# Input projection of a four-branch decoder layer: one Strassen level over blocks of 1024 tokens, columns passed on through DRAM

## The chip, the core and the metric

The kernel runs on one core of one Trainium2 chip. The metric is the device time of one execution in microseconds (us); three runs of the kernel before gave a median of 2729.23 us (2728.61 to 2731.78).

## The reference

One layer of a decoder on 2048 tokens of width 1024, all in float32:

```python
h = _rmsnorm(x, norm_pre)
cols = h @ w_in                      # (2048 x 1024) @ (1024 x 9992)
(dn_qkv, dn_z, dn_b, dn_a, gm_uv, gm_z, sw_q, sw_k, sw_v, sw_z, xm_q, xm_z, gate_logits) = _split_cols(cols)
mem_kv = _rmsnorm(mem, norm_mem) @ w_mem_kv
y_a = _deltanet_branch(dn_qkv, dn_z, dn_b, dn_a, ...)   # conv, silu, chunked delta rule with a state that runs over the tokens
y_b = _spatial_gating_branch(gm_uv, gm_z, ...)          # gelu, 128x128 mixing of positions
y_c = _sliding_window_branch(sw_q, sw_k, sw_v, sw_z, sinks)
y_m = _memory_branch(xm_q, xm_z, mem_kv)                # attention to 256 memory tokens
proj = jnp.einsum("btnc,ncd->btnd", jnp.stack([y_a, y_b, y_c, y_m], axis=2), w_up)
merged = jnp.sum(jax.nn.sigmoid(gate_logits.reshape(B, T, 4, D)) * proj, axis=2)
return x + _rmsnorm(merged @ w_out, norm_post)
```

Of the 9992 columns of the projection 8 belong to the two small gates of the DeltaNet branch; the other 9984 are 78 tiles of 128 columns (32 of them gate logits).

## The kernel before

**Products.** Each float32 matrix is split into a high part (rounded to fp32r, a cast on ScalarE) and a low part (the difference, a subtraction on VectorE or GpSimd); a product is three matmuls, high by high, low by high and high by low (`mac3`, L259). A matmul has 128 rows, 128 columns and 512 tokens.

**Passes.** The tokens go through in four passes of 512 (`for p in range(NPASS)`, L1146). In a pass the normalised input `hhi`, `hlo` (L350) stays in SBUF. Two tiles of 128 columns at a time are projected by `proj2` (L264): two units of weights (512 KB each) are loaded, split (`wunit`, L228) and multiplied, 48 matmuls in all. The result is taken from PSUM by the branch that wants it, at once: it never leaves SBUF.

**Order of the work.** The program is written with generators. A foreground generator (`fg`, L105) projects or multiplies; at each of its `yield`s every background generator (`start`, L114) goes one step. So the emission of the slow chains is spread over the foreground: `proj2` yields every 12 matmuls. The compiler then orders the instructions of each engine by readiness with the emission order as priority; buffers with one tag are handed out in the order of the program.

**The DeltaNet chain.** `dn_step` (L593) and `dn_scan` (L732) run per pass and per pair of heads (`q` = 0, 1): norms of keys and queries, the 32x32 triangular systems written to DRAM and read back in another layout (L661, L669), their solution by 32 pairs of a multiplication and a reduction on VectorE (L675, L676), written out and read back (L683, L686), the assembly of the 128x128 inverses, and a scan over four chunks in which each needs the state `S` of the one before. It has two PSUM buffers of its own (`dnp`, L80). Eight such chains run, each in the background of a good part of a pass's projections: chain 0 beside `branch_b`, `branch_c_kv`, `branch_c_q` and `gates_up(1)`, chain 1 beside `gates_up(2)` and others.

**The up projection.** `gates_up(n)` (L422) projects the 8 gate tiles of branch n, multiplies the branch's output by `w_up[n]` and adds the gated product to `merged`. After the fourth, `out_proj` (L1074) multiplies by `w_out`; the next pass's `phase_h` (L463) runs beside it.

Of the kernel before, what the change touches and what calls it, by code (L numbers as in the profile page):

```python
# [20 lines left out]
NB = TB // P  # L21
H = 4
EPS = 1e-6
NW, NWR = 6, 3
NS = 7
NT, NC, ND, NE = 12, 4, 11, 6
# [11 lines left out]
def trunk(tc, x, mem, norm_pre, norm_post, norm_mem, w_in, conv_w, a_log, dt_bias, dn_norm,  # L38
# [4 lines left out]
    NPASS = x.shape[0] // TB  # L43
# [5 lines left out]
    hp = pool("h", 1)  # L49
    wp = pool("w", 3)  # L50
# [3 lines left out]
    dp = pool("scr", 2, space=DRAM)  # L54
# [4 lines left out]
    def ctmp(name, dt=F32):  # L59
        return tp.tile([P, 512], dt, name=name, tag="c", bufs=NC)  # L60

    def dtmp(name, dt=F32):
        return tp.tile([P, 512], dt, name=name, tag="d", bufs=ND)

    def etmp(name, dt=F32):
        return tp.tile([P, 256], dt, name=name, tag="e", bufs=NE)

    def junk():
        return tp.tile([P, 512], BF16, name="junk", tag="e", bufs=NE)
# [15 lines left out]

    def load_rows(src, name, tmp):
        xt = [tmp(f"{name}x{i}") for i in range(2)]
        for i in range(2):
            nc.sync.dma_start(xt[i], src[:, i * 512:(i + 1) * 512])
        return xt  # L90

    first_rows = [load_rows(x[t * P:(t + 1) * P], "x", dtmp) for t in range(NB)]


# [10 lines left out]
    def fg(gen):  # L105

        try:
            while True:
                next(gen)
                step()  # L110
        except StopIteration as e:
            return e.value
# [26 lines left out]
    def wait(n):  # L139
        for _ in range(n):  # L140
            yield


# [21 lines left out]
    sel = cp.tile([P, 4, 4], F32R, name="sel")  # L165
    sel_f = small("sel_f", 16)
    V.memset(sel_f, 1.0)
    G.affine_select(sel_f.rearrange("p (i j) -> p i j", i=4), sel_f.rearrange("p (i j) -> p i j", i=4),
                    [[1, 4], [-1, 4]], ALU.is_equal, 0.0, base=0, channel_multiplier=0)
    V.tensor_copy(sel, sel_f.rearrange("p (i j) -> p i j", i=4))  # L170
# [22 lines left out]
    inv = cp.tile([P, 8, P], F32, name="inv")  # L193
    ud4 = dp.tile([4, 8, 32], F32, name="ud4", tag="ud4", bufs=1)


    def late_constants():
# [17 lines left out]
        tc.keep_in_program_order(G.memset(inv, 0.0))  # L215
# [9 lines left out]
    nsplit, solving = [0], []  # L225
    ON_DVE = ("gu", "gv", "gz", "az", "xq", "xz", "gate0", "gate2", "gate3", "u0", "u2", "u3", "wo")

    def wunit(src, name, k=4, swap=False, tags=None):  # L228


        raw = wp.tile([P, 1024], F32, name=f"{name}raw", tag="wraw", bufs=NWR)
        for d, s in (src if isinstance(src, list) else [(slice(None), src)]):
            nc.sync.dma_start(r3(raw, k)[d], s)
        res = []
        pl, th, tl, bufs = tags or (wp, "whi", "wlo", NW)
        for i in range(2):
            hi = pl.tile([P, 512], F32R, name=f"{name}hi", tag=th, bufs=bufs)
            lo = pl.tile([P, 512], F32R, name=f"{name}lo", tag=tl, bufs=bufs)
            rw = raw[:, i * 512:(i + 1) * 512]
            nsplit[0] += 1  # L240
            eng = V if name in ON_DVE or nsplit[0] % 3 == 0 and not solving else G
            if swap:
                perm = lambda t: t.rearrange("p (k a b c) -> p k b a c", k=2, a=2, b=2)
                same = lambda t: t.rearrange("p (k a b c) -> p k a b c", k=2, a=2, b=2)
                for kk in range(2):
                    A.copy(same(hi)[:, kk], perm(rw)[:, kk])
                    eng.tensor_tensor(same(lo)[:, kk], perm(rw)[:, kk], same(hi)[:, kk].bitcast(F32), op=ALU.subtract)
            else:
                A.copy(hi, rw)  # L249
                ins = eng.tensor_tensor(lo, rw, hi.bitcast(F32), op=ALU.subtract)  # L250
                if nsplit[0] < 5:
                    tc.keep_in_program_order(ins)
            res.append((r3(hi, k // 2), r3(lo, k // 2)))
        return lambda j: (res[j // (k // 2)][0][:, j % (k // 2)], res[j // (k // 2)][1][:, j % (k // 2)])
# [4 lines left out]
    def mac3(ps, lh, ll, rh, rl, first, last):  # L259
        T.matmul(ps, lh, rh, start=first, stop=False)  # L260
        T.matmul(ps, lh, rl, start=False, stop=False)  # L261
        T.matmul(ps, ll, rh, start=False, stop=last)  # L262

    def proj2(src, name, done, rh=None, rl=None, n=TB, swap=False):  # L264

        rh, rl = (hhi, hlo) if rh is None else (rh, rl)
        pss = [mm(name), mm(name)]
        for j in range(2):
            unit = wunit(src(j), name, swap=swap)
            for i in range(2):  # L270
                for k in range(4):
                    hi, lo = unit(k)
                    kk = 4 * j + k
                    mac3(pss[i][:, :n], hi[:, i * P:(i + 1) * P], lo[:, i * P:(i + 1) * P], rh[:, kk], rl[:, kk],
                         kk == 0, kk == KT - 1)
                if j:
                    done(i, pss[i])
                yield

    def cols_of(w, col):  # L280
        v = kview(w[:, col:col + 2 * P])
        return lambda j: v[:, 4 * j:4 * j + 4]
# [953 lines left out]
```

## Time and profile before

| | |
|---|---|
| median of three runs | 2729.23 us |
| profiled execution | 2728.63 us, span 2726.9 us |
| TensorE (PE) busy | 2684.6 us, 98% |
| VectorE (DVE) busy | 1546.7 us, 57% |
| ScalarE (ACT) busy | 1105.2 us, 41% |
| GpSimd (POOL) busy | 682.2 us, 25% |
| DMA | 271.29 MB, 34% of 16 engines' time |

The span goes from the first to the last instruction of the profiled execution. Matmuls are pipelined: each is recorded for longer than the distance to the next one, so the busy time of PE says that matmuls were in flight, and the distance of two starts says what one costs.

### The profile page before, as it was taken

What the parts mean: (1) busy time and instruction counts of PE and PEld (TensorE: products, weight loads), DVE (VectorE), ACT (ScalarE), POOL (GpSimd) and SP (SyncE); (2) the same over time, 40 slices, a digit from 0 to 9 for tenths busy, and PEclk for the clock granted to TensorE, in tenths of its full rate; (3) what the DMA queues carried; (4) which work ended last, traced back from release to release, by engine and by line L of the source; (5) the groups of instructions that cost most, each with busy time, mean ns of one, the idle gap of its engine ahead of it and who ended that gap; (6) DMA issues with size and microseconds to landing.
All of it is one profiled execution on the core that took longest, in us unless ns stands there. A gap on an engine that the chain in (4) does not pass through costs nothing. (4 is left out here: it accounts for less than half of the span.)

```text
span 2726.9 us, 37167 instructions
## 1 busy us (share of the span) xinstructions
PE 2684.6 (98%) x13453; PEld 2176.5 (80%) x13453; DVE 1546.7 (57%) x3355; ACT 1105.2 (41%) x2484; POOL 682.2 (25%) x689
## 2 busy tenths in 40 slices
PE   7989999999999999999999999999999999999998
PEld 5868777888888877888878887788887877778887
DVE  7464377544557547754465656665447455675444
ACT  5524343334453444343444334434344443433332
POOL 3333322011224332101223433210113334221111
PEclk9989999999999999999999999999999999999999
DMA  4342333224433233323533323332343332333242
GB/s 136 103 118 86 93 93 86 85 85 137 143 89 104 76 93 87 100 70 93 170 102 94 104 78 85 103 91 71 108 155 116 88 96 74 89 95 89 78 123 93
DMA packets 268015, 271.29 MB, mean 99 GB/s; under 512 B 33264, under 2 KB 238648, under 8 KB 267832
## 3 DMA queue, kind: packets, MB, share of 16 engines
q1 hardware_dynamic: 267656, 268.89, 34.1%
q8 instruction: 106, 1.74, 0.3%
q14 instruction: 77, 0.63, 0.1%
q10 hardware_dynamic: 80, 0.03, 0.0%
q0 software_dynamic: 96, 0.01, 0.0%
HBM read 251.31 MB, written 12.06 MB: 97 GB/s over the span
## 5 line engine op out<-in xcount | busy, mean ns | idle before, releaser
L455 POOL TENSOR_TENSOR merged<-merged,gp 128x512 f32<-128x512 f32 x96 | 138.7, 1445 | 685.2 <-DVE gp L454 670.4
L675 DVE TENSOR_TENSOR pr<-L,U 128x8 f32<-128x8 f32 (+31 forms) x256 | 102.0, 398 | 44.2 <-DMA L<-scr 37.4
L431 ACT ACTIVATE gt<-gate 128x512 f32<-128x512 f32 x128 | 76.2, 595 | 122.1 <-PE gate L262 121.8
L260 PE MATMUL gate<-hhi,gate1hi 128*128 128x512 f32 x256 | 105.9, 414 | 0.0
L260 PE MATMUL gate<-hhi,gate2hi 128*128 128x512 f32 x256 | 102.3, 400 | 0.0
L260 PE MATMUL wo<-wohi,mh 128*128 128x512 f32 x256 | 102.0, 399 | 0.0
L260 PE MATMUL gate<-hhi,gate3hi 128*128 128x512 f32 x256 | 100.8, 394 | 0.0
L261 PE MATMUL gate<-hlo,gate1hi 128*128 128x512 f32 x256 | 100.5, 393 | 0.0
L262 PE MATMUL gate<-hhi,gate1lo 128*128 128x512 f32 x256 | 100.5, 393 | 0.0
L262 PE MATMUL wo<-wohi,ml 128*128 128x512 f32 x256 | 100.0, 391 | 0.0
L261 PE MATMUL gate<-hlo,gate2hi 128*128 128x512 f32 x256 | 100.0, 391 | 0.0
L261 PE MATMUL gate<-hlo,gate3hi 128*128 128x512 f32 x256 | 100.0, 391 | 0.0
L260 PE MATMUL gate<-hhi,gate0hi 128*128 128x512 f32 x256 | 99.9, 390 | 0.0
L262 PE MATMUL gate<-hhi,gate2lo 128*128 128x512 f32 x256 | 99.9, 390 | 0.0
L262 PE MATMUL gate<-hhi,gate3lo 128*128 128x512 f32 x256 | 99.8, 390 | 0.0
L261 PE MATMUL wo<-wolo,mh 128*128 128x512 f32 x256 | 99.6, 389 | 0.0
L261 PE MATMUL gate<-hlo,gate0hi 128*128 128x512 f32 x256 | 99.6, 389 | 0.0
L262 PE MATMUL gate<-hhi,gate0lo 128*128 128x512 f32 x256 | 99.6, 389 | 0.0
L250 DVE TENSOR_TENSOR gate0lo<-gate0raw,gate0hi 128x512 fp32r<-128x512 f32 x64 | 44.0, 692 | 94.7 <-ACT gate0hi L249 94.7
L454 DVE SCALAR_TENSOR_TENSOR gp<-gt,up 128x512 f32<-128x512 f32 x96 | 65.6, 683 | 54.0 <-PE up L262 53.2
L250 POOL TENSOR_TENSOR gate1lo<-gate1raw,gate1hi 128x512 fp32r<-128x512 f32 x48 | 62.1, 1301 | 125.8 <-ACT gate1hi L249 125.7
L250 DVE TENSOR_TENSOR gate3lo<-gate3raw,gate3hi 128x512 fp32r<-128x512 f32 x64 | 44.3, 692 | 81.7 <-ACT gate3hi L249 81.7
(483 smaller groups left out, 8272.8 us busy)
## 6 DMA issues: line engine op xcount, KB each, us to landing
gate1raw<-in_w_in_dram SPq DMA_DIRECT2D x32, 512.0 KB, 3.6
gate2raw<-in_w_in_dram SPq DMA_DIRECT2D x32, 512.0 KB, 3.6
gate3raw<-in_w_in_dram SPq DMA_DIRECT2D x32, 512.0 KB, 3.6
gate0raw<-in_w_in_dram SPq DMA_DIRECT2D x32, 512.0 KB, 3.7
woraw<-in_w_out_dram SPq DMA_DIRECT2D x32, 512.0 KB, 3.8
xx<-in_x_dram SPq DMA_DIRECT2D x32, 256.0 KB, 5.1
dn0raw<-in_w_in_dram SPq DMA_DIRECT2D x16, 512.0 KB, 3.6
dn1raw<-in_w_in_dram SPq DMA_DIRECT2D x16, 512.0 KB, 3.7
```

What stands on the lines that cost most here:

```text
L250: ins = eng.tensor_tensor(lo, rw, hi.bitcast(F32), op=ALU.subtract)
L260: T.matmul(ps, lh, rh, start=first, stop=False)
L261: T.matmul(ps, lh, rl, start=False, stop=False)
L262: T.matmul(ps, ll, rh, start=False, stop=last)
L431: A.activation(t, ps, AF.Tanh, scale=0.5)
L454: V.scalar_tensor_tensor(g, ts[d2], 1.0, ps, op0=ALU.add, op1=ALU.mult)
L455: G.tensor_tensor(merged[:, d], merged[:, d], g, op=ALU.add)
L675: V.tensor_tensor(pv, L[:, i, i:32].unsqueeze(1).broadcast_to([P, 8, n]), U[:, :, i:32], op=ALU.mult)
```

## The change

**Blocks.** The tokens go through in two blocks of 1024 (`BLK`), each of two sub-blocks `s` of 512. A product of the block's input (two halves of tokens by two halves of the 1024 inputs) and of a *quad* of weights (two halves of the inputs by two tiles of 128 columns) is one level of Strassen's scheme in Winograd's form: seven products of halves where there were eight. There are 39 quads a block; a product of halves is 4 `mac3`, 12 matmuls.

**Left operands.** `phase_h` makes the transposed, scaled input of both sub-blocks, four sums of its quarters on POOL, and the split of seven operands (A11, A12, A22, S1 to S4), which take 56 buffers of 128x512 for the whole projection of a block. There is now one tag of 77 such buffers for nearly everything.

**Weights.** `Weights.load` reads four quarters (256 KB each, rows of 512 B) two quads ahead, `sums` makes four sums on POOL, and `split` splits one of seven operands two products ahead.

**Results.** The four outputs of a quad are put together from four PSUM banks by one copy (ACT) and five additions (DVE), pass through their first function (tanh, gelu, silu, or the convolution and silu of the DeltaNet's columns) and are written to a DRAM scratch (`put`). The branches, which start when all 39 quads of a block are done, read them back (`get`).

**After the projection.** `branch_b`, the DeltaNet chains (now `dn_chain`, the four of a block one after the other), the sliding window and the memory attention are the background of `up(1)`, `up(2)` and `up(3)` alone, which yield every 6 matmuls. `up(0)` and `out_proj` follow once the chains are finished. The weights `w_up` are loaded and split once a block. In the very last half of `out_proj` the weights are loaded three times.

**Smaller edits.** Row sums of squares of keys and queries by one fp32 matmul, not two of fp32r; softmax of the memory branch scaled on ACT, not on DVE; gMLP's `v` transposed on PE, as it comes with the columns on partitions; the second sub-block's rows of `x` wait for four buffers of their own tag; every other weight split outside the projection on POOL.

```diff
+NT, NX = 77, 4
...
+    def phase_h(b, gts):
+        L = {n: [None] * 4 for n in ("A11", "A12", "A22", "S1", "S2", "S3", "S4")}
...
+                for n, u, v, op in (("S1", "A21", "A22", ALU.add), ("S3", "A11", "A21", ALU.subtract),
+                                    ("S2", "S1", "A11", ALU.subtract), ("S4", "A12", "S2", ALU.subtract)):
...
+                    G.tensor_tensor(t, val(u), val(v), op=op)
...
+    def put(name, s, t):
+        nc.sync.dma_start(cols[name][:, s * TB:(s + 1) * TB], t)
...
+    class Weights:
...
+        def sums(self):
+            B11, B12, B21, B22 = self.r
+            t1, t2, t4 = (r3(tmp(n), 4) for n in ("T1", "T2", "T4"))
+            G.tensor_tensor(t1, B12, B11, op=ALU.subtract)
+            G.tensor_tensor(t2, B22, t1, op=ALU.subtract)
+            G.tensor_tensor(t4, B21, t2, op=ALU.subtract)
+            G.tensor_tensor(B12, B22, B12, op=ALU.subtract)
...
+    PRODUCTS = (("X", "A11", "B11"), ("Y", "S2", "T2"), ("W", "S3", "T3"), ("Z", "S1", "T1"),
+                ("X", "A12", "B21"), ("Z", "S4", "B22"), ("W", "A22", "T4"))
+    AHEAD = 2
+    def project(b, left, quads, ws):
...
+            bank = (lambda i: mm(f"q{i}")) if q % 2 == 0 else (lambda i: (att if i < 2 else dnp)(f"q{i}"))
...
+            for i, (p, a, w) in enumerate(PRODUCTS):
...
+                for k in range(4):
+                    ah, al = left[a][k]
+                    mac3(ps[p], hi[:, k], lo[:, k], ah, al, new and k == 0, k == 3, not new)
+                if i == 0 and q + 2 < len(ws):
+                    ws[q + 2].load()
+                if i == 3 and q + 1 < len(ws):
+                    ws[q + 1].sums()
+                q_, i_ = (q, i + AHEAD) if i + AHEAD < 7 else (q + 1, i + AHEAD - 7)
+                if q_ < len(ws):
+                    ws[q_].split(PRODUCTS[i_][2])
+                if i == 0:
+                    e1 = tmp("e1")
+                    A.copy(e1, ps["X"])
+                elif i == 1:
+                    u2 = tmp("u2")
+                    V.tensor_tensor(u2, ps["Y"], e1, op=ALU.add)
+                elif i == 3:
+                    u4 = tmp("u4")
+                    V.tensor_tensor(u4, ps["Z"], u2, op=ALU.add)
+                    o = sink.place(1, 1)
+                    V.tensor_tensor(o, ps["W"], u4, op=ALU.add)
+                    sink.done(1, 1, o)
...
+    def dn_chain(b, gts):
+        for s in range(SB):
+            for q in range(2):
+                p = b * SB + s
+                st = yield from dn_load(p, q, gts[s])
+                yield from dn_step(st)
+                on_of[p, q] = st
...
+    for b in range(NBLK):
...
+        fg(project(b, left, quads, ws))
...
+        cb = start(chain_b())
+        dn = start(dn_chain(b, gts))
+        cc = start(chain_c(b, yc))
+        finished(cb)
+        fg(up(b, 1, merged, yb))
+        finished(cc)
+        cm = start(chain_m(b, ym))
+        ca = start(chain_a(b, dn, ya))
+        fg(up(b, 2, merged, yc))
+        finished(cm)
+        fg(up(b, 3, merged, ym))
+        finished(dn, ca)
...
+        fg(up(b, 0, merged, ya, out_split))
...
+        for s in range(SB):
+            if b + 1 < NBLK and s == 1:
+                hb = start(phase_h(b + 1, gts))
+            fin = fg(out_proj(b * SB + s, mh[s], ml[s]))
```

## Rows read from the trace of the kernel before

**Rows 1.** The page, busy time, share and instructions of each engine.
```profile
PE 2684.6 (98%) x13453; PEld 2176.5 (80%) x13453; DVE 1546.7 (57%) x3355; ACT 1105.2 (41%) x2484; POOL 682.2 (25%) x689
```
**Rows 2.** Timeline of PE in a projection: start us, us recorded, line and operation.
```profile
2201.70 0.39 PE L261 MATMUL sz<-hlo,szhi 128*128 128x512 f32 x1
...
2205.80 0.39 PE L261 MATMUL sz<-hlo,szhi 128*128 128x512 f32 x1
```
**Rows 3.** Timeline of PE at the start: first transposes, first matmul of a projection.
```profile
8.34 1.11 PE L342 MATMUL xtp<-ident,xx 128*128 128x128 f32 x4 [8.34 <-DVE xx L328]
...
23.56 0.40 PE L260 MATMUL dn<-hhi,dn0hi 128*128 128x512 f32 x1
```
**Rows 4.** Groups of instructions, DVE: count, busy us, mean ns, idle before.
```profile
L675 DVE TENSOR_TENSOR pr<-L,U 128x8 f32<-128x8 f32 (+31 forms) x256 | 102.0, 398 | 44.2 <-DMA L<-scr 37.4
L676 DVE TENSOR_REDUCE U<-pr 128x8 f32<-128x8 f32 (+31 forms) x256 | 74.4, 291 | 6.9
L454 DVE SCALAR_TENSOR_TENSOR gp<-gt,up 128x512 f32<-128x512 f32 x96 | 65.6, 683 | 54.0 <-PE up L262 53.2
L250 DVE TENSOR_TENSOR gate3lo<-gate3raw,gate3hi 128x512 fp32r<-128x512 f32 x64 | 44.3, 692 | 81.7 <-ACT gate3hi L249 81.7
...
L542 DVE SCALAR_TENSOR_TENSOR dn0a<-dn,ccol,dn0a 128x509 f32<-128x509 f32 (+2 forms) x48 | 35.6, 741 | 35.9 <-ACT dn0a L539 35.4
...
L954 DVE COPY_PREDICATED sc<-gt_mask,scp 128x256 f32<-128x256 uint32 x60 | 23.9, 442 | 35.2 <-ACT sc L953 35.2
...
L1030 DVE TENSOR_REDUCE xm<-xs 128x2 f32<-128x512 f32 x32 | 21.9, 685 | 11.2 <-PE xs L262 11.0
...
L753 DVE SCALAR_TENSOR_TENSOR R<-ks,neg_eg,dv 128x128 f32<-128x128 f32 x64 | 19.4, 345 | 6.8 <-PE ks L750 5.9
...
L773 DVE SCALAR_TENSOR_TENSOR S<-S,eg,sps 128x128 f32<-128x128 f32 x64 | 19.3, 343 | 23.6 <-PE sps L770 23.5
```
**Rows 5.** Groups of instructions, POOL and ACT.
```profile
L250 POOL TENSOR_TENSOR gate1lo<-gate1raw,gate1hi 128x512 fp32r<-128x512 f32 x48 | 62.1, 1301 | 125.8 <-ACT gate1hi L249 125.7
...
L637 POOL TENSOR_TENSOR gtri<-triu,gr 128x256 fp32r<-128x256 f32 x64 | 49.8, 803 | 79.2 <-PE dps L642 51.4 <-DVE gr L531 25.6 <-DVE gr L532 2.1
...
L249 ACT CAST gate3hi<-gate3raw 128x512 fp32r<-128x512 f32 x64 | 39.9, 624 | 57.8 <-PE gate L261 42.3 <-PE az L261 9.6 <-DVE gate3lo L250 5.9
```
**Rows 6.** One chain, second of eight, by stage: busy us in each stretch, clock, DMA.
```profile
388.00:429.00 41.00, 40.46 (x225) 31.40 (x224) 24.60 (x56) 15.80 (x45) 10.74 (x16) 1.00 0.32 94
429.00:437.00 8.00, 8.00 (x42) 6.75 (x41) 5.99 (x15) 2.65 (x10) 2.43 (x2) 1.00 0.44 132
437.00:466.00 29.00, 29.00 (x128) 23.26 (x128) 27.29 (x75) 9.61 (x18) 3.17 (x3) 1.00 0.30 74
466.00:475.00 9.00, 9.00 (x59) 7.24 (x59) 4.18 (x8) 2.31 (x4) 1.29 (x1) 1.00 0.61 158
475.00:493.00 18.00, 18.00 (x155) 14.19 (x150) 10.97 (x15) 6.57 (x13) 4.70 (x3) 1.00 0.31 88
493.00:537.00 44.00, 44.00 (x244) 37.87 (x244) 24.95 (x62) 16.36 (x46) 2.10 (x3) 1.00 0.26 74
```
**Rows 7.** A stretch in which PE waited, and the two after it (columns as in Rows 6).
```profile
170.00:180.00 10.00, 3.11 (x13) 1.93 (x11) 6.35 (x13) 3.43 (x8) 4.56 (x4) 0.78 0.81 227
180.00:190.00 10.00, 9.92 (x88) 6.57 (x89) 3.04 (x8) 2.73 (x7) 1.41 (x2) 0.50 0.29 88
190.00:200.00 10.00, 10.00 (x52) 8.36 (x51) 2.03 (x6) 0.58 (x1) 0.00 (x0) 0.53 0.20 52
```
**Rows 8.** DMA: a queue's share of 16 engines, and issues with KB and us to landing.
```profile
q1 hardware_dynamic: 267656, 268.89, 34.1%
...
gate1raw<-in_w_in_dram SPq DMA_DIRECT2D x32, 512.0 KB, 3.6
xx<-in_x_dram SPq DMA_DIRECT2D x32, 256.0 KB, 5.1
...
L<-scr SPq DMA_DIRECT2D x8, 512.0 KB, 4.9
```

More of the change, by code (lines that the diff above doesn't have):

```diff
@@ L53, in trunk @@
     pp = pool("ps", 1, space=PSUM)
-    dp = pool("scr", 2, space=DRAM)
+    dp = pool("scr", 1, space=DRAM)
     def tmp(name, dt=F32):
@@ L110, in fg, with run @@
                 step()
+        except StopIteration as e:
+            return e.value
+    def run(gen):
+        try:
+            while True:
+                next(gen)
         except StopIteration as e:
@@ L518, in dn_gates @@
                         nexpa.unsqueeze(1).broadcast_to([P, NB, H]), op=ALU.mult)
-        for _ in range(9):
-            yield
+        yield from wait(2)
         gps = dnp("gps")
@@ new lines, in chain_a, with branch_b, rows @@
+    def chain_a(b, dn, ya):
+        for s in range(SB):
+            for q in range(2):
+                while (b * SB + s, q) not in on_of:
+                    yield
+                yield from branch_a(b * SB + s, q, ya[s])
+    def branch_b(b, s, ys):
+        gvt = [get(("gv", i, b), s) for i in range(4)]
+        vs = [None] * NB
+        yield
+        def rows(t):
+            tps = att("gvt")
+            for i in range(4):
+                T.transpose(tps[:, i * P:(i + 1) * P], gvt[i][:, t * P:(t + 1) * P], ident)
@@ new lines, in rows, with mix @@
+            yield
+            A.activation(vs[t], tps, AF.Copy, scale=r)
+            yield
+        yield from staggered([rows(t) for t in range(NB)], 1)
+        def mix(g):
+            u, sz = get(("gu", g, b), s), get(("gz", g, b), s)
+            sps = att("gs")
+            for c in range(NB):
+                T.matmul(sps[:, c * P:(c + 1) * P], vs[c][:, g * P:(g + 1) * P], wsT[:, g], start=True, stop=True)
+            G.tensor_tensor(sz, sz, u, op=ALU.mult)
+            yield
+            V.scalar_tensor_tensor(r3(u, NB), r3(sps, NB), g_gm[:, g:g + 1],
+                                   bsb[:, g * P:(g + 1) * P].unsqueeze(1).broadcast_to([P, NB, P]),
+                                   op0=ALU.mult, op1=ALU.add)
+            yield
+            V.tensor_tensor(u, u, sz, op=ALU.mult)
+            yield
+            ys.append(ysplit(u, "yb"))
@@ L972, in block @@
             G.tensor_tensor(scv, scv, den.unsqueeze(2).broadcast_to([P, 4, P]), op=ALU.mult)
-            yield from wait(4)
+            yield from wait(2)
             tps = att("ptp")
@@ L980, in block @@
             V.tensor_tensor(r3(prv, 4), r3(tps, 4), slow.unsqueeze(1).broadcast_to([P, 4, P]), op=ALU.mult)
-            yield from wait(2)
+            yield
             cv = cur.rearrange("p (i a q) -> p a i q", i=2, a=2)
@@ L1074, in out_proj, with chain_m @@
-    def out_proj(p, merged, mh, ml):
+        ys.append(ysplit(sz, "ym"))
+    def chain_m(b, ym):
+        t = {}
+        for n in mks:
+            t[n] = tmp("mk" + n, F32 if n[0] == "v" else F32R)
+            nc.sync.dma_start(t[n].bitcast(F32), mks[n])
+        yield from wait(2)
+        kv = ([t[f"h{h // 2}"][:, (h % 2) * MEM:(h % 2 + 1) * MEM] for h in range(H)],
+              [t[f"l{h // 2}"][:, (h % 2) * MEM:(h % 2 + 1) * MEM] for h in range(H)], [t["v0"], t["v1"]])
+        for s in range(SB):
+            for h in range(H):
+                yield from branch_m(b, s, h, kv, ym[s])
@@ new lines, in finish @@
+            for half in range(2):
+                nc.sync.dma_start(out[rows, half * 512:(half + 1) * 512], xs[t][half])
+    quads = quad_list()
+    nc.sync.dma_start(bar, kview(w_in[:, OFF_BA:OFF_BA + 8]), allow_slow_non_contiguous=True)
+    A.copy(baw[:, :, 0:8], bar)
+    V.tensor_tensor(baw[:, :, 8:16], bar, baw.bitcast(F32)[:, :, 0:8], op=ALU.subtract)
+    lc = start(late_constants())
+    gts = [{}, {}]
+    hb = start(phase_h(0, gts))
+    fg(mem_kv())
+    left = finished(hb)
+    finished(lc)
```

977 lines of the change are left out of this document (456 added, 521 removed).

## The prediction

> **What bounds the kernel now.** I read the page's busy shares first: TensorE is busy 98% of the span, DVE 57%, ACT 41%, POOL 25% [rows 1]. Then the timeline of PE, since a busy PE need not be a full one: in a projection 18 matmuls of 512 tokens take 4.10 us, 0.228 us each, with no gap [rows 2]. The reader is to see that PE is the bound nearly everywhere: 7488 such matmuls are the projection (78 tiles x 24 x 4 passes), 1536 the up projection and 768 `out_proj`, together 9792 x 0.228 = 2233 us; the rest of PE's 2684.6 us, 452 us, is the branches' small work and the transposes, and 42 us of the span are idle. Last I read one DeltaNet chain stage by stage [rows 6]: it takes 149 us, in which PE is busy 148.5 us, mostly with projections. The chain is long, but hidden.
>
> **The saving.** Seven products of halves for eight: 39 quads x 84 matmuls x 2 blocks = 6552, where there were 7488. 936 x 0.228 = 213 us of PE.
>
> **The projection of a block.** 3276 x 0.228 = 747 us, if PE stays the bound. Beside a quad's 19.2 us of PE stand 7 splits and 5 additions on DVE, 12 x 0.69 = 8.3 us (by the split of gate3lo, [rows 4]); a DeltaNet quad adds 12 multiply-adds of the convolution at 0.74 (L542, [rows 4]) and 4 for its silu, 8.9 + 2.8 = 11.6 us more, 19.9 in all, just over PE's, but there are 6 among 39 and what they leave over is worked off in the next quad. ACT has 7 casts, a copy and 4 first functions, 12 x 0.62 = 7.4 us [rows 5], and POOL 4 sums of 1.3 us, 5.2 us [rows 5]. All of it lies beside PE. Two waits are new on PE: the sixth product adds onto a bank that DVE must have read after the fourth, so DVE has one product, 2.7 us, for it, and what is queued before it on DVE are splits of 0.69 us. On SP's queue each `put` waits for its result and holds back the weights behind it, which have a quad's time to spare. The buffers are tight: of 77, 56 are held by the left operands, and the 28 allocations of a quad hold 18.6 on average (lifetimes counted in products from the diff), where 21 are free. I add 8 us a block for late splits (0 to 30): 755 us. DMA: 4 weight quarters are as many bytes per quad as before per pair of tiles and pass, 82 MB less in all, `w_up` 17 less; the columns add 82 MB each way: 268.89 becomes some 334 MB, and the 34.1% [rows 8] some 42%. No bound.
>
> **After the projection.** Here is what the change moves. The branches had the whole pass as cover; now what runs beside a block's four chains is `up(1)` to `up(3)`, 576 matmuls, 131 us, and the branches' own PE work, at most 452 / 2 = 226 us, I take 200: 331 us a block. The chains run one after the other, as they share two PSUM buffers and the state; `up(0)` and `out_proj` wait for the last. Call this stretch W. Three things bound it:
>
> PE: 331 us. DVE: the lines of the chain sum to 355 us (19 lines; the solve's two are 102.0 + 74.4, the scan's R and S 19.4 + 19.3 [rows 4]), the window attention 182 (from L954, 23.9 [rows 4], down), the memory attention 68 (from L1030, 21.9 [rows 4], down), gMLP and the output of A 66, `up` 83 (two thirds of L454 [rows 4], the first sum, 24 splits): 754, a block's half 377 us. The chains: 4 times one.
>
> One chain before takes 41 us for norms and triangular systems, 8 for their way through DRAM (the load alone lands in 4.9 us [rows 8]), 29 for the solve, 9 for the way back, 18 for the inverses, 44 for the scan [rows 6]. That is an upper bound, for it was paced by the foreground: some 60 steps, each behind 12 matmuls (2.7 us). From below: the solve's busy time, 176.4 / 8 = 22 us [rows 4]; the two DMA trips, 8 + 6 us, stay; the first stage has 10.7 us of POOL in that row, twice that with what comes before and after, 21; the inverses are half copies and waits, 9; a chunk of the scan needs two of R, two of S (4 x 0.34 [rows 4]) and three rounds of small matmuls with a hand-over each, some 4.5 us, 18 in all. Sum 84 us. Between 84 and 149 I take 110: the solve at 29 and the DMA trips at 17 as they were, since DVE will be over 80% busy and the trips don't change, and the remaining 103 us down to 64, because a step now stands behind 6 matmuls (1.4 us) and not 12, but behind a fuller DVE. So W = 440 us a block (from 377, DVE's bound, to 4 x 149 = 596). PE is idle about 110 us of it. That is the price: 2 x 110 us, as large as the saving. The next thing late is DVE.
>
> **Start, change of block, end.** Before, the first projection began at 23.6 us [rows 3]. Now 1024 tokens have to be there: rows of the second sub-block wait for four buffers until the first is transposed (some 27 us), land 12 us later (an estimate from 5.1 us per 256 KB load [rows 8], several at once), 6 us for norms, then four rounds of 10 DVE operations of 0.69, 28 us: 75 us (60 to 95), in which PE has the memory keys. At the change of block the same four rounds stand behind an `out_proj` that covers most of it: 15 us (5 to 30). The end, three loads of the last weights: 10 us, where it was some 7. `up(0)` and `out_proj` follow W: 192 + 384 matmuls, 131 us a block, and 12 us before them for the last chain's output, its transposes and splits.
>
> **The sum.** 75 + 2 x (755 + 440 + 12 + 131) + 15 + 10 = 2776 us of span; the profiled execution before was 1.7 us over its span and 0.6 us under the median of the runs. Forecast 2778 us, 1.8% slower. Its own range, chains of 104 to 125 us: 2730 to 2900.
>
> The smaller edits have one answer: fp32 squares, `v`'s transposes, the halved loads of `w_up`, splits moved to POOL, softmax scaling on ACT move a few us between engines of which, in W, only DVE counts, and are in its 377 us.
>
> **Rivals.** *The chains are hidden, PE or DVE bounds W.* For it: the minima sum to 84 us, 4 x 84 = 336 < 377; and DVE can run nearly full (27.29 of 29 us in the solve's row [rows 6]). Against: the one chain read took 149 us, and DVE would have to be full for 377 us while the chain's hand-overs, each waiting for the one before, go through it. W = 377 to 405 gives 2652 to 2708, point 2670; with PE the bound (331) 2560.
>
> *The clock.* Where PE had been busy for 3.11 of 10 us, the granted clock of the next 20 us was 0.50 and 0.53, half of 2.4 GHz [rows 7]. In W PE has work for 75% of the time and gaps at each DMA trip and solve. Four chains with two such gaps each, 20 us at half clock each, lose 8 x 10 = 80 us of PE's work a block; 110 us of W are idle anyway, but the chains' own small matmuls and what is queued before them slow down too. It decides if the clock falls at each of these gaps, as it did there, and what is lost falls on the chains' path. W = 440 + 80: 2938. The Trainium skill, "TensorE: Matmul & The Clock Gate", section "Part 1: The HAM clock gate", says that half rate is the default and only activity lifts it. The trace agrees as far as it goes: after that one gap 0.5. By that rule alone a W at half clock throughout would be PE's, 2 x 331 = 662 us, and the kernel 3220 us; a PE that is then full would get its clock back, so I give it no more than this rival's chance.
>
> *The change doesn't do what it says:* the 21 free buffers or the one-product deadline on DVE hold PE up once a quad by one product, 2.7 us: 78 x 2.7 = 213 us, all that was saved. Speaks for it that 21 against 18.6 leaves little; against it that splits are two products ahead. 2776 + 197 = 2975.
>
> **Chances.** Forecast 0.45, hidden chains 0.33, clock 0.10, held up in the projection 0.07; the seam between the first two, where W = 413 to 418 and nothing can be told from no change (0.2%, 5.5 us, is what a measurement of this kernel can tell), 0.05. So faster 0.33, same 0.05, slower 0.62. The range, 2610 to 2940, leaves out the fully PE-bound W below and the worst of the last two above.
>
> **What would show it.** In the profile after: PE full in the projection's slices, starts 0.228 us apart; two stretches of 400 to 500 us in which PE falls to some 70 to 75% and DVE is the busiest it gets; PE's idle time there put down to the lines of solve, scan and their DMAs; the first product at 75 us. PE's busy time some 200 us lower, its idle time over 250 us. Wrong, if W is under 400 us (chains overlap more than I see, or hand-overs are quicker), or if PE has gaps inside the projection.

## The result and the profile after

The changed kernel takes 3513.58 us (median of four runs, 3511.67 to 3514.34), the one before 2728.92 us beside it: 1.287 times as long (interval 1.285 to 1.290). Slower was forecast, but 2778 us and at most 2940. The page of after, busy times, then the 40 slices of PE and of its clock:

```profile
PE 2803.5 (80%) x12581; PEld 2172.7 (62%) x12581; DVE 1865.1 (53%) x3507; ACT 1087.1 (31%) x2427; POOL 1001.7 (29%) x872
...
PE   6699999999757686667759999999995676755776
...
PEclk8799999999868687888869999999997787877887
```

Against [rows 1] PE has 872 matmuls fewer and is recorded busy for 119 us more: recorded durations grow at half clock (0.39 us in [rows 2], 0.63 in the row at 245.28 us shown with the convolution below). The slices show two full stretches (the projections) and behind each a stretch in which PE's digits lie between 5 and 8. The first block by stages (windows: busy us of PE, PEld, DVE, ACT, POOL with counts, granted clock, DMA share, GB/s):

```profile
0.00:126.00 126.00, 68.53 (x283) 48.57 (x283) 81.35 (x163) 51.98 (x115) 53.17 (x52) 0.76 0.38 118
126.00:926.00 800.00, 766.76 (x3282) 625.41 (x3282) 448.57 (x643) 281.63 (x484) 222.91 (x152) 0.97 0.34 99
926.00:1578.00 652.00, 434.12 (x2232) 309.78 (x2232) 341.74 (x870) 172.97 (x541) 170.82 (x196) 0.77 0.29 89
1578.00:1650.00 72.00, 53.31 (x192) 41.55 (x192) 22.42 (x35) 13.23 (x23) 24.45 (x19) 0.83 0.34 111
1650.00:1785.00 135.00, 104.54 (x434) 82.87 (x434) 60.15 (x93) 44.67 (x102) 39.78 (x33) 0.87 0.31 107
1785.00:1840.00 55.00, 21.77 (x71) 10.59 (x69) 47.61 (x92) 17.02 (x39) 29.35 (x20) 0.57 0.33 96
```

These are the start, the projection, the stretch W of the branches, `up(0)`, `out_proj` and the change of block. In W, the longest addition, nothing is full: PE 67%, DVE 52%, ACT 27%, POOL 26%. The four chains in it, by PE's first matmul of each and the first of `up(0)` (timeline of PE in after: start us, us recorded, operation, in brackets the idle time before it and who ended it):

```profile
934.93 1.87 PE L662 MATMUL ssp<-sq,sel 128*4 128x512 f32 x2 [2.60 <-POOL sq L660]
...
1142.47 1.02 PE L662 MATMUL ssp<-sq,sel 128*4 128x512 f32 x2
...
1293.54 1.88 PE L662 MATMUL ssp<-sq,sel 128*4 128x512 f32 x4
...
1435.12 1.87 PE L662 MATMUL ssp<-sq,sel 128*4 128x512 f32 x2
...
1578.12 0.80 PE L253 MATMUL up<-yah,u0h 128*128 128x512 f32 x1 [4.35 <-ACT u0h L233]
```

They follow each other by 208, 151, 142 and 143 us, 161 on average, where 110 was forecast. The chain of [rows 6] is a shorter stretch: it begins at the copy of the sums of squares (388.14 us) and ends with the last addition of the scan. Between these two marks the chains take 166, 112, 126 and 124 us here (timelines of ACT and DVE):

```profile
951.55 0.57 ACT L671 COPY srow<-ssp 4x512 f32<-4x512 f32 x1 [1.40 <-PE ssp L662]
1116.93 0.41 DVE L847 TENSOR_TENSOR on<-on,sps 128x256 f32<-128x256 f32 x1
...
1151.89 0.58 ACT L671 COPY srow<-ssp 4x512 f32<-4x512 f32 x1 [1.00 <-PE ssp L662]
1263.92 0.41 DVE L847 TENSOR_TENSOR on<-on,sps 128x256 f32<-128x256 f32 x1
...
1299.61 0.58 ACT L671 COPY srow<-ssp 4x512 f32<-4x512 f32 x1 [3.90 <-PE ssp L662]
1425.07 0.41 DVE L847 TENSOR_TENSOR on<-on,sps 128x256 f32<-128x256 f32 x1
...
1446.63 0.57 ACT L671 COPY srow<-ssp 4x512 f32<-4x512 f32 x1 [1.08 <-PE ssp L662]
1570.49 0.42 DVE L847 TENSOR_TENSOR on<-on,sps 128x256 f32<-128x256 f32 x1
```

That is 132 us on average, where the chain read before took 149. Outside these marks lie 26 us before the first chain, 35, 35 and 21 between them and 7 behind the last. The other work of W ends at nearly the same time as the chains, with the last matmul of `up(3)` (timeline of PE):

```profile
1563.47 0.39 PE L255 MATMUL up<-ymh,u3l 128*128 128x512 f32 x1
```

### The profile page after: what moved, and what is told of

It reads as the page before. It is cut to its first block, busy times and chain, and to the rows that moved or that the text cites. A ratio compares the mean times of both kernels' runs of the same rounds, so it can differ in the third digit from the quotient of the medians.

```text
span 3510.0 us, 37990 instructions
## 1 busy us (share of the span) xinstructions
PE 2803.5 (80%) x12581; PEld 2172.7 (62%) x12581; DVE 1865.1 (53%) x3507; ACT 1087.1 (31%) x2427; POOL 1001.7 (29%) x872
## 3 DMA queue, kind: packets, MB, share of 16 engines
q1 hardware_dynamic: 349448, 338.96, 31.8%
## 5 line engine op out<-in xcount | busy, mean ns | idle before, releaser
L1156 POOL TENSOR_TENSOR ggate<-ggate 128x512 f32<-128x512 f32 x96 | 125.7, 1309 | 216.7 <-DVE ggate L1154 206.0
L253 PE MATMUL q<-S2h,T2h 128*128 128x512 f32 x312 | 134.2, 430 | 62.3 <-ACT T2h L233 62.3
L525 POOL TENSOR_TENSOR B<-B,B 128x512 f32<-128x512 f32 x78 | 132.8, 1703 | 0.0
L254 PE MATMUL q<-S2l,T2h 128*128 128x512 f32 x312 | 131.9, 423 | 0.0
L255 PE MATMUL q<-S2h,T2l 128*128 128x512 f32 x312 | 131.8, 422 | 0.0
L255 PE MATMUL q<-A11h,B11l 128*128 128x512 f32 x312 | 125.0, 401 | 2.7 <-DVE B11l L234 1.6
L253 PE MATMUL q<-A11h,B11h 128*128 128x512 f32 x312 | 125.0, 401 | 1.6 <-ACT B11h L233 1.6
L254 PE MATMUL q<-A11l,B11h 128*128 128x512 f32 x312 | 123.5, 396 | 0.0
L253 PE MATMUL q<-S3h,T3h 128*128 128x512 f32 x312 | 122.9, 394 | 0.0
L254 PE MATMUL q<-S3l,T3h 128*128 128x512 f32 x312 | 122.3, 392 | 0.0
```

Source lines behind the costliest of these rows:

```text
L253: T.matmul(ps, lh, rh, start=first, stop=False, skip_group_check=more)
L254: T.matmul(ps, lh, rl, start=False, stop=False, skip_group_check=more)
L255: T.matmul(ps, ll, rh, start=False, stop=last, skip_group_check=more)
L525: G.tensor_tensor(B12, B22, B12, op=ALU.subtract)
L1156: G.tensor_tensor(merged[s][d], merged[s][d], t, op=ALU.add)
```

## The experiments

Theory A: the four chains in series set W. Theory B: several branches, each a series of hand-overs (one engine waits for what another has made), wait for one another in the engines' in-order queues, and the chains lie beside. Theory C: SyncE's one queue holds transfers back. Later theory E: PE's in-order queue is the path, its work and its waits add up. The first block's stages in each run, from the starts of its matmuls (first product; projection; W; `up(0)` and `out_proj`; change of block), and the median time:

```
                 start  proj.   W    up0+out  change   time us
after             126    799   653     207      55     3513.6
e1_no_chain       125    798   471     204      55     3139.2
e2_no_solve       126    799   604     204      55     3414.2
e3_conv_steps     128    771   655     207      55     3457.5
e4_eight           99    884   662     206      31     3639.0
e5_chain_only     126    798   487     204      55     3183.9
e6_pool_queue     126    799   654     205      55     3512.9
e7_together       127    799   653     207      55     3506.0
e8_two_chains     126    800   628     200      55     3432.5
e9_unit_ahead     125    798   631     194      59     3457.5
e10_keep_busy     126    798   688     208      55     3582.0
e11_room          132   1065   181     202      62     3105.0
e12_three         127    781   631     172      59     3360.6
e13_leads         126    797   679     206      55     3560.3
e14_three_more    126    771     837 in all     59     3409.2
e15_up_third      125    798   625     179      55     3388.2
```

**No chains.**
```diff
-                st = yield from dn_load(p, q, gts[s])
-                yield from dn_step(st)
-                on_of[p, q] = st
+                yield
+                on_of[p, q] = 0
...
```


> Leaves out the DeltaNet chains (their loads, triangular systems, solve and scan); branch A's output is its gate alone. The kernel after has 650 us a block between the last product and up(0). Theory A (the four chains, one after the other, are what those 650 us consist of): without them the stretch falls to what PE and DVE have left there, 380 to 420 us, and the run takes about 3030 us. Theory B (the other branches' work and the up projections run one behind the other in the in-order queues, and the chains lie beside them): the stretch stays above 550 us, the run above 3310 us.

3139.2 us, ratio to before 1.151 (1.148 to 1.154), between the two. 182 us of W go, but what stays is no engine's time either (windows, W of that run):
```profile
923.00:1394.00 471.00, 323.02 (x1193) 219.77 (x1192) 177.90 (x390) 136.98 (x410) 93.37 (x76) 0.71 0.32 103
```
PE 69%, DVE 38%: the other branches and the up projections are a series of hand-overs of their own, as long as the one forecast for the chains.

**No solve.**
```diff
+            if i == 31:
                 V.tensor_tensor(pv, L[:, i, i:32]..., U[:, :, i:32], op=ALU.mult)
                 V.tensor_reduce(U[:, :, i], pv, AX.X, ALU.add, negate=True)
```


> Leaves out 31 of the 32 steps of each triangular solve (62 of 64 DVE operations), with the same number of hand-overs to other work. Theory A (the chain is the path): each of 8 chains is shorter by its solve, about 30 us, so 240 us less, about 3270 us. Theory B (the chain lies beside): at most a third of that, 3430 us or more.

3414.2 us, 1.252 (1.248 to 1.255): 99 us less, 12.4 a chain. DVE's busy time in W falls by 76 us (341.74 to 266.20), W by 49, two thirds of it. The edit relieves DVE and shortens the chains at once; which of the two gave the 49 us it can't tell.

**Chains only.**
```diff
+        for g in range(4):
+            sz = get(("gz", g, b), s)
+            yield
+            ys.append(ysplit(sz, "yb"))
+        return
         gvt = [get(("gv", i, b), s) for i in range(4)]
...
```


> The counterpart of the run without chains: gMLP, window attention and memory attention are left out (a quarter of their columns goes to the up projections as it is), the four chains and all up projections stay. Without chains the stretch between the last product and up(0) was 471 us, with everything 653. If a chain's own steps are what takes its 114 to 171 us, it stays above 125 us alone, the stretch above 500, the run above 3210 us. If it is mostly held up by the other branches' work in the same in-order queues, a chain takes 85 to 105 us alone, the stretch 350 to 430, the run 2920 to 3080 us; then 471 and some 400 lie so little beside each other that together they take 653.

3183.9 us, 1.168 (1.164 to 1.172), W 487 us: just under the one expectation, well over the other. The chains in it (timeline of PE, as above):
```profile
928.76 1.87 PE L662 MATMUL ssp<-sq,sel 128*4 128x512 f32 x2 [4.58 <-POOL sq L660]
...
1086.17 1.02 PE L662 MATMUL ssp<-sq,sel 128*4 128x512 f32 x2 [0.65 <-POOL sq L660]
...
1218.94 1.86 PE L662 MATMUL ssp<-sq,sel 128*4 128x512 f32 x2
...
1311.54 1.87 PE L662 MATMUL ssp<-sq,sel 128*4 128x512 f32 x2
...
1410.79 0.79 PE L253 MATMUL up<-yah,u0h 128*128 128x512 f32 x1 [5.64 <-ACT u0h L233]
```
157 and 133 us beside the up projections, 93 and 99 beside nothing (they end at 1201). So a chain has about 95 us of its own; what it takes beyond that it takes beside other work. Between the marks of [rows 6] the four chains take 131, 122, 82 and 85 us in this run. 487 and 471 us, run together, take 653: a third of the shorter one is paid. Both hold the same up projections, so of what the other branches add to them the paid share is larger.

**The queue of the transfers.**
```diff
-                nc.sync.dma_start(scr[c * 2:c * 2 + 2, b]...
+                G.dma_start(scr[c * 2:c * 2 + 2, b]...
```


> The 16 small writes of each chain's triangular systems go to GpSimd's queue in the place of SyncE's, where they waited 149 us in all for GpSimd in the first block's stretch, with weights and columns queued behind them. Theory C (one queue for all transfers holds back weights and columns): half of that comes back, 2 x 75 us, about 3360 us. Rival (what is queued behind is early enough): within 30 us of 3514.

3512.9 us, 1.288 (1.285 to 1.292), no change. But the edit moved the wait and did not take it away: the read of `L`, which stayed on SyncE's queue, now waits for these writes to land (waits of SP in W: us in total, times, longest; after, then this run):
```profile
SPq L732 <- POOL m L729: 149.2, 15, 35.3
```
```profile
SPq L739 <- DMA scr<-m: 106.6, 12, 31.9
```
All waits of that queue in W sum to 503 us in after and to 535 in this run, and ACT waits 57 and 51 us for the weights of `up(3)`. So theory C is neither shown nor refuted; it stays open.

**Memory attention from the start.**
```diff
-            sps = att("xs")
+            sps = mm("xs")
...
         cc = start(chain_c(b, yc))
+        cm = start(chain_m(b, ym))
         finished(cb)
...
```


> Memory attention starts with the other branches, in PSUM banks that only the up projections use, and not after window attention is done. Theory B (phases in series): PE's foreground no longer waits 119 us a block between up(2) and up(3), the stretch is shorter by 80 to 119 us, the run 3280 to 3350 us. Theory A (the chains set the end): no more than 20 us a block, 3475 us or more.

3506.0 us, 1.286 (1.282 to 1.290), as theory A expected. The wait of 118 us between `up(2)` and `up(3)` went (8 us there now), and most of it came back in front of `up(0)`: W is 653 as before. The last matmul of `up(3)` now lies 91 us earlier than in after, but the last chain does not (timelines of PE and DVE):
```profile
1472.52 0.39 PE L255 MATMUL up<-ymh,u3l 128*128 128x512 f32 x1
...
1569.62 0.41 DVE L847 TENSOR_TENSOR on<-on,sps 128x256 f32<-128x256 f32 x1
```
Here the chains end the stretch. Phases in series are not enough to explain it; that form of theory B falls.

**Two chains side by side.**
```diff
+        bank = (dnp, mm)[q]
...
-        for s in range(SB):
-            for q in range(2):
...
+        yield from staggered([one(0), one(1)], 8)
```


> Heads 0, 1 and heads 2, 3 of the DeltaNet go as two chains side by side, the second one in the up projections' PSUM banks (75 buffers for 77, one more of the large ones). The four chains in series took 171 + 114 + 128 + 132 = 545 us with 87 us between them. Theory A: their series is halved, the stretch falls to what the other branches need, 471 to 520 us, the run to 3150 to 3250 us. Theory B: the waits for the other branches stay, the stretch loses 60 us at most, the run takes 3390 us or more.

3432.5 us, 1.259 (1.255 to 1.263): inside what theory B expected. Half the series is taken away and W gives back 25 and 46 us (blocks one and two). The chains are done early, 191 us earlier than in after (last addition of the last chain, timeline of DVE):
```profile
1379.75 0.41 DVE L850 TENSOR_TENSOR on<-on,sps 128x256 f32<-128x256 f32 x1
```
`up(0)` begins at 1554 us even so: memory attention, which starts when window attention is done, and `up(3)` behind it now end the stretch. This edit and the one before each free one of the two series and leave the other. The two in one kernel were not run.

**Convolution in steps.**
```diff
-                        self.conv(h, s_)
+                        convs.append(start(self.conv(h, s_)))
...
+            yield from wait(2)
             t = tmp("acct")
...
```


> The convolution of a DeltaNet quad is issued step by step between later work, the splits of weights ahead of it, instead of all at once. A projection takes 799 us, 52 more than 3276 matmuls at 0.228 us, and PE has one gap of 5.2 us and a spell at half clock for each of the 6 DeltaNet quads. Theory: ACT's in-order queue is held by the convolution and the cast of the next weights waits behind it; then both projections fall to about 750 us, the run to about 3410 us. Rival: buffers are short and the cast waits for one; then the gaps stay, and the time within 20 us of 3514.

3457.5 us, 1.268 (1.264 to 1.271): half of what was expected. What it mends is seen in after, in one DeltaNet quad (timelines of ACT, then of PE):
```profile
235.53 0.72 ACT L473 ACTIVATE acc<-cv,ccol 128x512 f32<-128x512 f32 x1
239.37 0.63 ACT L480 ACTIVATE acct<-acc 128x512 f32<-128x512 f32 x1 [3.12 <-DVE acc L475]
239.91 0.70 ACT L473 ACTIVATE acc<-cv,ccol 128x512 f32<-128x512 f32 x1
243.07 0.63 ACT L480 ACTIVATE acct<-acc 128x512 f32<-128x512 f32 x1 [2.46 <-DVE acc L475]
243.60 0.60 ACT L233 CAST T2h<-T 128x512 fp32r<-128x512 f32 x1
```
```profile
238.64 0.39 PE L255 MATMUL q<-A11h,B11l 128*128 128x512 f32 x1
244.26 0.79 PE L253 MATMUL q<-S2h,T2h 128*128 128x512 f32 x1 [5.23 <-ACT T2h L233]
244.85 0.63 PE L254 MATMUL q<-S2l,T2h 128*128 128x512 f32 x1
245.28 0.63 PE L255 MATMUL q<-S2h,T2l 128*128 128x512 f32 x1
```
The cast of T2 stands in ACT's queue behind three of the quad's four tanh, each of which waits for three DVE operations; PE waits 5.2 us and then goes at 0.43 us a matmul for a while. In steps the clock stays up throughout (windows of that run; the clock is the 1.00):
```profile
128.00:900.00 772.00, 752.10 (x3282) 615.33 (x3280) 442.42 (x638) 280.71 (x483) 224.82 (x152) 1.00 0.35 102
```
What is left over 747 us are three short waits of PE a DeltaNet quad for DVE's low halves (18.4 us in all, the longest 1.6), so DVE is late there as well.

**Eight plain products.**
```diff
-    PRODUCTS = (("X", "A11", "B11"), ("Y", "S2", "T2"), ("W", "S3", "T3"), ("Z", "S1", "T1"),
-                ("X", "A12", "B21"), ("Z", "S4", "B22"), ("W", "A22", "T4"))
+    PRODUCTS = (("00", "A11", "B11"), ("01", "A21", "B11"), ("10", "A11", "B12"), ("11", "A21", "B12"),
+                ("00", "A12", "B21"), ("01", "A22", "B21"), ("10", "A12", "B22"), ("11", "A22", "B22"))
...
```


> Eight plain products in the place of the seven, in the otherwise same arrangement (blocks of 1024 tokens, quads of products, columns through DRAM, the same work after the projection); no sums of halves on either side. 39 x 2 x 12 = 936 matmuls more, 213 us of PE. If the seven products save what PE has less: 3514 + 213 = 3727 us, less what the sums cost now at the start and in the stalls (up to 51 at the start and 2 x 52 in the projections), 3560 to 3730 us. If the sums eat the saving: 3514 us or less.

3639.0 us, 1.334 (1.330 to 1.338), 125 more than seven. Seven for eight is worth 85 us a block in the projection; the sums and splits of the left halves take 27 us back at the start and 24 at the change of block. So 125 of the 213 us are saved, and the new order of the work costs 3639 - 2729 = 910.

**Weights one unit ahead.**
```diff
+            gates, unit = nxt.pop((n, dp_))
...
+                nxt[n_, d_] = up_unit(b, n_, d_)
...
```


> The weights of up and out_proj are loaded and split one unit earlier, ahead of the products, gates and splits that ACT's in-order queue now has in front of their cast. up(0) takes 69 us for 44 of matmuls, out_proj 132 for 88, up(1) to up(3) 95 each. Theory (the cast waits behind work that waits for PE, as with the convolution): up(0) and out_proj lose 40 to 65 us a block, up(1) to up(3) 20 each, the run takes 3270 to 3380 us. Rival (half clock, evacuation): within 40 us of 3514.

3457.5 us, 1.268 (1.264 to 1.271), less than expected. In after PE stood still 5.4 us before each weight unit (timeline of PE in `up(0)`):
```profile
1596.24 0.79 PE L253 MATMUL up<-yah,u0h 128*128 128x512 f32 x1 [5.40 <-ACT u0h L233]
```
That goes. But `up(0)` still takes 70 us: it now begins before the last chain has ended (1554 us, chain to 1578), and that chain's scan and its transposes run in between. `out_proj` takes 124 for 132: there the next block's transposes hold PE up (8.5 us in one place, 11.1 in after). Since the border between W and `up(0)` has moved, the two and `out_proj` are best taken together: they lose 35 and 22 us (blocks one and two).

**PE kept busy.**
```diff
     def step():
+        if warm:
+            ps = mm("warm")
+            for _ in range(3):
+                T.matmul(ps, warm[0][:, 0:P], warm[0], start=True, stop=True)
...
```


> Between the last product and up(0), PE gets three matmuls of 512 columns more (their result is not used) at every hand-over between branches. The granted clock in that stretch was 0.77 on average, PE was busy 434 us there, some 100 of them by the half clock. If the half clock costs time there: the clock rises, the stretch loses 60 to 100 us, the run takes 3310 to 3390 us. If it does not lie on the path: the extra matmuls only add, 3514 us or more.

3582.0 us, 1.313 (1.309 to 1.317). W of that run:
```profile
924.00:1612.00 688.00, 559.64 (x2945) 420.29 (x2944) 341.82 (x872) 173.19 (x541) 169.39 (x196) 0.89 0.28 85
```
713 matmuls more, 163 us at 0.228, lengthen W by 36 us, and the clock rises from 0.77 to 0.89. The Trainium skill, "TensorE: Matmul & The Clock Gate", section "Part 1: The HAM clock gate", has activity lift the throttle; the rise agrees. But the time does not fall: what the clock returns and what the added work costs (its time on PE, and the PSUM bank that it shares with the up projections) can't be told apart here, so the half clock's own price stays open.

**Longer leads.**
```diff
-        yield from wait(4)
+        yield from wait(10)
...
+                if (s, hf) != (SB - 1, 1):
+                    ahead = start(branch_c_q(b, s + hf, 1 - hf))
```


> Two leads, counted in hand-overs, are made longer: the solve's way back through DRAM gets 10 hand-overs for 4 before PE's next matmul on it, and the queries of the next half of window attention are prepared while this one's blocks run. PE waited 32 us for the former (z from lt) and 31 us for the latter (scp from sq) in the first block's stretch of 652 us. Theory E (PE's in-order queue is the path: its work, 434 us at the clock that it has, and each wait in it add up): the two waits go, 2 x 63 us, about 3390 us. Theory A or B (the chains or the phases set the end): within 25 us of 3514.

3560.3 us, 1.305 (1.301 to 1.309): 47 us worse, against every theory. The wait for the solve's way back seems to have grown (waits of PE in W: us in total, times, longest; after, then this run):
```profile
PE z L768 <- DMA lt<-scu: 32.0, 4, 10.9
PE scp L1008 <- DMA sq<-sql: 30.8, 8, 11.1
```
```profile
PE z L768 <- DMA lt<-scu: 54.7, 3, 29.0
```
But 29.0 of the 54.7 us are one wait, of the fourth chain (timeline of PE in this run):
```profile
1531.09 0.39 PE L255 MATMUL up<-ymh,u3l 128*128 128x512 f32 x1
1560.44 1.06 PE L768 MATMUL z<-lt,m 32*32 32x32 f32 x32 [28.96 <-DMA lt<-scu]
```
`up(3)` is done, and PE stands through that chain's whole solve with nothing left to do beside it. The 31 us for `sq` are gone from the list, and yet W grew: between the marks of [rows 6] the first two chains took 25 and 28 us longer than in after, the last two 8 and 10 less. Which of the two leads did it was not taken apart.

**Leads, steps and units together.**
```diff
-        yield from wait(4)
+        yield from wait(10)
...
-                        self.conv(h, s_)
+                        convs.append(start(self.conv(h, s_)))
...
+                nxt[n_, d_] = up_unit(b, n_, d_)
```


> The longer leads, the convolution in steps (alone 56 us less) and the weights one unit ahead (56 us less) together, with one chain at a time. Theory E: the sum of the three, 3514 - 56 - 56 - 126 = 3276 us; if the leads are worth nothing, 3400 us.

3409.2 us, 1.250 (1.246 to 1.253): what the steps and the units give (3514 - 112 = 3402), and nothing for the leads.

**A third of the up projections.**
```diff
-                        mac3(ps, hi[:, d2 * P:(d2 + 1) * P], lo[:, d2 * P:(d2 + 1) * P],
-                             ys[s][c][0], ys[s][c][1], c == 0, c == 3)
+                        T.matmul(ps, hi[:, d2 * P:(d2 + 1) * P], ys[s][c][0], start=c == 0, stop=c == 3)
```


> The up projections keep one of their three passes (the high halves; the two with a low half are left out), with the same loads, splits, hand-overs and evacuations. In the stretch after the projection PE has 384 matmuls of 512 columns less, 88 us at 0.228, and up(0) 128 less, 29 us; PE is busy 67% of that stretch, so by busy shares alone nothing should follow there. Theory E (PE's queue is the path): 2 x (88 + 29) = 234 us less, about 3280 us. Theory A (the chains set the end and the ups lie beside them): up(0) alone, 2 x 29, about 3455 us.

3388.2 us, 1.242 (1.238 to 1.246): 125 us less, between the two. W loses 28 and 38 us of the 88 that PE has less, so a third of PE's work counts there:
```profile
924.00:1535.00 611.00, 363.95 (x1829) 251.34 (x1830) 325.31 (x856) 169.18 (x532) 167.27 (x194) 0.70 0.29 90
```

**Room.**
```diff
-                        L[n][j] = hi, lo
+                        L[n][j] = hi, hi
...
+                    split(sums[n], V, n)
+                    L[n][j] = L["A11"][j]
...
+            bank = lambda i: mm(f"q{i}")
+            if q in later:
+                later[q]()
...
+            7: lambda: gen.update(dn=start(dn_chain(b, gts))),
+            13: lambda: gen.update(bcm=start(bcm())),
```


> What would be if there were room: the projection takes turns in four PSUM banks in the place of eight; of the left operands' 56 buffers 12 are kept (all sums read A11, low halves read the high ones, their own are computed and dropped), DeltaNet's quads come first, and the four chains and the other branches start beside the projection as soon as their columns are written. The up projections read a stand-in and not the branches' results, so that these need no buffers. Theory (what is lost is the projection as a cover): the projection grows by the branches' work on PE, at most 226 us a block, the 653 us after it shrink to the up projections, 210 to 280 us; 2850 to 3100 us in all. Rival (the hand-overs hold up PE's in-order queue just as much beside the projection): 3350 us or more.

3105.0 us, 1.138 (1.135 to 1.142), 5 us above the theory's range. W shrinks from 653 to 181 us, the projection grows by 266. Both, by windows:
```profile
132.00:1197.00 1065.00, 982.04 (x4791) 767.59 (x4792) 715.93 (x1389) 399.04 (x905) 325.71 (x293) 0.95 0.36 106
1197.00:1377.00 180.00, 163.62 (x725) 125.96 (x724) 68.22 (x122) 47.41 (x127) 61.07 (x47) 0.98 0.49 153
```
With a projection to stand behind, the same hand-overs leave PE 92% busy. Of the 785 us lost 409 come back, although this is no kernel: it needs the buffers that the left operands hold, and its up projections wait for no branch, which is part of the 409.

**Three edits that worked, together.**
```diff
+        yield from staggered([one(0), one(1)], 8)
...
-                        self.conv(h, s_)
+                        convs.append(start(self.conv(h, s_)))
...
+                nxt[n_, d_] = up_unit(b, n_, d_)
```


> Three together: convolution in steps (alone 56 us less), two chains side by side (81 us less), weights one unit ahead. If each acts on its own wait, the sum: about 3514 - 137 - 190 = 3190 us. If they are after the same time, 3300 us or more.

3360.6 us, 1.232 (1.226 to 1.238): 153 us less, where the three alone gave 56 + 81 + 56 = 193. It is the fastest whole variant, and 23% slower than the kernel before.

## Why the prediction was wrong

The forecast's span against after's, both blocks: start 51 us more, projections 2 x 44, W with the end of the last chain 201 + 201, `up(0)` and `out_proj` 76 + 79, change of block 40, end 2 less. Sum 734 = 3510 - 2776.

*W, 402 of the 734.* The step that failed is "W = 440 us a block (from 377, DVE's bound, to 4 x 149 = 596)", with the chains as "4 times one". Measured are 528 us in the four chains and 124 outside their marks, 653 in all. So a chain took 132 us for the 110 of the sum, 88 of the 201 us a block. Another 117 lie before and between the chains: the loads, the squares and their matmuls stand ahead of the stretch that [rows 6] show, and the sum had no term for them. (The end took 7 us for 12.)

Without the other branches the four chains took 420 us where 440 were forecast, so the chain by itself was sized well; what lengthens it is its company. Before, a step stood behind 12 matmuls, which wait for nothing [rows 2]. After, it stands behind other branches' steps, which wait themselves. I had taken the largest of three terms, PE 331, DVE 377 and the chains, and counted the other branches by busy time alone. They are a fourth term: with the up projections they take 471 us without any chain. Two such series overlap badly, 653 and not 487. DVE's busy time was near (342 for 377); PE's was 434 for 331, recorded at a mean clock of 0.77. The upper bound, 149 a chain, was not far off for the chains as such (166 for the first, less for the others; the eight before took 149 to 168 by the same marks); it was none for W, which holds what lies between them too.

No single resource sets W, and neither series alone. Taking DVE work out of the chains gave two thirds of it back, PE work in the up projections a third. With the chains' series halved, the other branches ended W (25 to 46 us back); with the other branches done earlier, the last chain ended it (0 and 4 us back). The Trainium skill, "Perfetto Trace Analysis", section "Identifying the Most-Contended Engine", says to optimize first the engine with the highest occupancy, and to judge TensorE by the busy share of its weight loads and not of its matmuls. In W the weight loads are busy for 48% and DVE for 52%, and the trace agrees with that order: 49 us came back for 76 of DVE, 28 and 38 for 88 of PE. Which queue makes the two series cost each other a third of the shorter stays open: A and B are both too simple, C was not tested, and E failed on the leads.

*The projection, 88.* The 19.9 us of DVE against 19.2 of PE for a DeltaNet quad were "worked off in the next quad" by busy time. The order in ACT's queue was not looked at. In steps 55 of the 88 us go (28 and 27); what remains there is DVE's late low halves. It is the rival of the held-up projection, with 12 waits of 5.2 us and not 78 of 2.7, and its cause was neither buffers nor the sixth product's bank.

*`up(0)` and `out_proj`, 155.* They were taken at 0.228 us a matmul and covered by nothing. The cast of the next weights stands behind work that waits for PE: 5.4 us of wait per unit, and a granted clock of 0.83 and 0.87 in these stages. A unit ahead gives back 13 and 4 us there (35 and 22 with W) and shifts the rest: the next block's transposes and the last chain are in the same queue. The remainder was not taken apart.

*Start and change of block, 91.* The four rounds on DVE were counted, at 28 us; DVE is busy for 81 of the first 126 us and for 48 of the 55. Without sums and splits of the left halves 51 us go.

*What held.* The sign, and its reason: the branches lost their cover. Given a cover, 409 us return, in a variant whose up projections wait for no branch. DMA's volume was near: 338.96 MB on the one large queue for some 334, 31.8% for some 42% (the span is longer). No stage of the first block has a share over 0.38, so DMA's throughput was no bound. The saving is there as well: PE's 936 matmuls are gone, 125 us of 213 arrive.

*The rivals.* Hidden chains: wrong, no chain was hidden. The clock: half clock is there as that rival had it (0.77 in W), but a higher one did not shorten W.

## What to carry to other kernels

Before a long matmul phase is finished ahead of the work that stood beside it, count that work a second time: not its busy time, but the length of each branch's series of hand-overs. If there are two such series, expect more than the longer one (here 487 and 471 gave 653), and look which of them ends last: time taken out of the other gives little. Time a chain from the end of the one before it, not from its first landmark: here 21 to 35 us of every chain lay in between. And when an operand's cast shares an in-order queue with an operation that waits for another engine, read the queue's order, not its share: ACT's held up PE here where it was busy for 35% (projection) and 27% (W) of the time.

## What the hardware showed that was not expected

A single wait of 5.2 us in an otherwise full PE is followed by matmuls 0.43 us apart, where 0.228 is usual [rows 2]. Windows of after around it (clock in the third column from the end):
```profile
238.00:245.00 7.00, 1.77 (x7) 1.03 (x5) 5.55 (x10) 3.00 (x5) 0.00 (x0) 0.89 0.10 37
245.00:252.00 7.00, 7.00 (x22) 5.51 (x21) 6.19 (x10) 2.76 (x5) 1.99 (x2) 0.62 0.74 203
252.00:262.00 10.00, 10.00 (x46) 8.29 (x45) 6.28 (x8) 3.88 (x7) 3.97 (x3) 1.00 0.19 67
```
0.62 is a mean of full and half clock (2.4 and 1.2 GHz); by 252 it is full again. PE's starts tell where (timeline of PE):
```profile
250.35 0.39 PE L255 MATMUL q<-S3h,T3l 128*128 128x512 f32 x1
```
From the first matmul behind the wait, at 244.26 us, to this one 14 matmuls are started in 6.09 us, where 14 x 0.228 = 3.2 us would do. So the wait of 5.2 us cost 2.9 us more than itself, and there are 12 such waits in this kernel. The waits of up to 1.6 us that remain with the convolution in steps leave the clock at 1.00.
